# Conformer layer of a hybrid decoder trunk: opening in half groups, second product with three blocks side by side, modulation vectors dealt out anew

## The chip, the cores and the metric

The kernel runs on one core of a Trainium2 chip. A core has five engines that run side by side and each take their own instructions in order: TensorE (PE; its weight loads are shown as PEld), VectorE (DVE), ScalarE (ACT), GpSimd (POOL) and SyncE (SP), which here issues nearly all transfers. Sixteen DMA engines move data between HBM and the on-chip memory SBUF; TensorE writes its results to PSUM, of which the kernel has eight banks. The metric is the time of one execution on the device in microseconds; lower is better.

## What is computed

Two layers over 256 tokens of width 2048. Layer 0 mixes tokens with a causal Conformer convolution, layer 1 with a Mamba-2 scan; a squared-ReLU MLP of width 8192 follows each. Every sub-layer is normalised, scaled, shifted and gated by vectors that come from the conditioning vector c through w_mod. Cut to what matters:

```python
sc = jax.nn.silu(c)
for i in range(DEPTH):
    mod = (sc @ w_mod[i] + b_mod[i])[:, None, :]
    sh1, sc1, g1, sh2, sc2, g2 = jnp.split(mod, 6, axis=-1)
    u = rmsnorm(h, norm_mix_g[i]) * (1 + sc1) + sh1
    mix = conformer_conv(u, ...) if i % 2 == 0 else mamba2(u, ...)
    h = h + g1 * mix
    u = rmsnorm(h, norm_mlp_g[i]) * (1 + sc2) + sh2
    h = h + g2 * sq_relu_mlp(u, mlp_w1[i], mlp_w2[i])
return rmsnorm(h, final_norm_g)

def conformer_conv(u, ...):
    a, gt = jnp.split(u @ w_pw1 + b_pw1, 2, axis=-1)
    v = causal_dwconv(a * jax.nn.sigmoid(gt), w_dw, b_dw)      # 31 taps
    v = jax.nn.silu(layernorm(v, ln_g, ln_b))
    return v @ w_pw2 + b_pw2
```

## The kernel before

**Layout.** Activations lie transposed: 2048 channels are four groups of four tiles of 128 partitions, each 256 tokens wide. Weights come in tiles of 1 MB (`load_w`, tag `w32`, three buffers): 512 rows of one group by 512 output columns, a block. The first product of the Conformer (`native`, L632) uses float32 directly; all others go through `split_w` (L329 to L340), which makes of each half tile a high part on ACT (L337) and a low part on DVE (L338), three buffers each, and `products` (L342) sums high by high, high by low and low by high.

**Vectors of w_mod.** `mod` of a layer is 6 segments (SH1, SC1, G1, SH2, SC2, G2) of 16 column tiles. A job `(layer, segment, column tile)` is one `gemv` (L243): a 1 MB transfer into a buffer of tag `wm` (two) or `hid` (four), in the turn that `self.rings` gives, then a product with silu(c). For groups in `PE_GROUPS` this is done by TensorE (four matmuls, L258; after four jobs the row is copied by ACT, L264, and turned into columns by `columns`, L279), for the others by DVE in one pass (L267). `mod_done` adds the bias on POOL. `pump(n)` takes n jobs off the list; the tables `RATE_...` say how many at each weight tile. `need` takes whatever is still missing at once.

**Order.** The program is written in one order and a scheduler places each engine's instructions by priority (`high_priority(n)` moves them n places ahead). `issue_after(ins)` keeps what is traced in the block behind `ins` on the engine of `ins`. `stream` keeps all loads of weights and vectors on SP in the order of the program, so a load that waits for a buffer holds all later ones.

**Stages that the change touches.**
- *Opening* (`native` with the first three blocks, L618 to L676): the scale and shift of a group (eight vectors, all on DVE) must be there before its input `u` can be made (`vectors`, L538) and multiplied by three blocks.
- *First product, blocks 3 to 7*, beside the convolution (`conv`: 24 taps on ACT, L565, the rest on DVE; the last two channel tiles have 13 taps on TensorE, L576) and the sums of the LayerNorm (`close`, `moments`). Jobs run by `RATE_PW1`.
- *LayerNorm* (L707 to L748): last sums (L718), mean and variance, and `v`, the normed input in four groups. The first weight tile of the second product is split before it. Six jobs (`BETWEEN`) are given to TensorE behind the sums.
- *Second product* (L762 to L770): four blocks one after the other, each over all four groups (`block`); results go into h (`into_h`, L790, squares L499, sums L496). Then four jobs of (0, SC2, 2), moved to the front by `first`, are put on TensorE.
- *MLP of layer 0* (`mlp`, L811): `outer` takes three blocks side by side, group by group, while the modulated input of a group is made (`modulate`, L502), with jobs by `RATE_OPEN`.
- *MLP of layer 1*: the same opening without jobs; then one job at each weight tile, but `to_rows` (L861), stepped from the first `block`, needs all that are left (`need(1, G2)`), and then turns h into rows (L870, L871) in two buffers of tag `wm` and spreads the gate (L881, L882).

Of the kernel before, what the change touches and what calls it, by code (L numbers as in the profile page):

```python
# [29 lines left out]
def spread(n, slots):  # L30
# [128 lines left out]
class Trunk:  # L159
# [83 lines left out]
    def gemv(self, layer, seg, ct, parts=((0, 4),)):  # L243
# [8 lines left out]
        if (layer, seg, g) in PE_GROUPS:  # L252

            if i == 0:
                self.row_sums = self.bank(*self.side)
# [5 lines left out]
            if i == 3:  # L261
                row = self.t("t2", [P, 512], bufs=3)
                with self.tc.issue_after(self.act) if self.act else nullcontext():
# [3 lines left out]
        nc.vector.scalar_tensor_tensor(out=w, in0=w, scalar=1.0, in1=self.scb, op0=ALU.mult,  # L267
                                       op1=ALU.mult, accum_out=m[:, i:i + 1])
# [15 lines left out]
    def mod_done(self, layer, seg, kg, i0=0, i1=4):  # L284
# [3 lines left out]
        nc.gpsimd.tensor_tensor(out=m, in0=m, in1=self.col("b_mod", (layer * 6 + seg) * NT + 4 * kg + i0, n),  # L288
                                op=ALU.add)
        if seg in (SC1, SC2):  # L290
            g = "norm_mix_g" if seg == SC1 else "norm_mlp_g"
            nc.gpsimd.tensor_scalar(out=m, in0=m, scalar1=1.0, scalar2=1.0, op0=ALU.add, op1=ALU.mult)
            nc.gpsimd.tensor_tensor(out=m, in0=m, in1=self.col(g, layer * NT + 4 * kg + i0, n), op=ALU.mult)
# [20 lines left out]
    def first(self, layer, seg, g):  # L314

        take = lambda j: j[0] == layer and j[1] == seg and j[2] // 4 == g
        self.jobs = [j for j in self.jobs if take(j)] + [j for j in self.jobs if not take(j)]

# [10 lines left out]
    def split_w(self, w):  # L329

        nc = self.nc
        out = []
        for i in range(2):
            s = slice(2 * i, 2 * i + 2)
            wh = self.wp.tile([P, 2, 512], F32R, tag="wh", name=self.nm("wh"), bufs=3)
            wl = self.wp.tile([P, 2, 512], F32R, tag="wl", name=self.nm("wl"), bufs=3)
            nc.scalar.copy(out=wh, in_=w[:, s, :])  # L337
            nc.vector.tensor_tensor(out=wl, in0=w[:, s, :], in1=wh.bitcast(F32), op=ALU.subtract)  # L338
            out.append((wh, wl))
        return out  # L340
# [15 lines left out]
    def block(self, src, rhs, evac, pump=None, single=False, ahead=None, there=()):  # L356
# [5 lines left out]
        for g in range(4):  # L362
            w, parts = there[g] if g < len(there) else (self.load_w(src[g]), None)
            if pump:
                self.pump(pump(g))
            if parts is None:
                with self.tc.high_priority(self.ahead if ahead is None else ahead):
                    parts = self.split_w(w)
# [44 lines left out]
    def outer(self, srcs, make, evac, pump):  # L413

        banks = [[self.bank(self.mm, "mm") for _ in range(2)] for _ in srcs]
        for g in range(4):
            x = make(g)
            for b, src in enumerate(srcs):
                w = self.load_w(src[g])
                with self.tc.issue_after(self.split):  # L420
                    self.pump(pump(g))
                with self.tc.high_priority(self.ahead):
                    parts = self.split_w(w)
# [90 lines left out]
    def conformer(self):  # L514
# [12 lines left out]
        nc.vector.reciprocal(r, r)  # L527
# [29 lines left out]
        def conv(ct):  # L557
# [5 lines left out]
            def products(p4, k):  # L563
                for q in range(4):
                    nc.scalar.activation(out=p4[:, q, :], in_=vp[:, k + q:k + q + T], func=AF.Identity,  # L565
                                         scale=self.col("w_dw", ct * TAPS + k + q),
# [660 lines left out]
```

## Time and profile before

| | us |
|---|---|
| three runs | 2635.2, 2631.5, 2634.6 |
| median | 2634.6 |
| profiled execution | 2634.52 |
| its span | 2632.7 |

The profile is of one execution. The page lists each engine's busy time, the busy share in 40 slices, the DMA queues and the chain of waits that ended last; other views give busy time by stretch, groups of instructions by line, waits, and the timeline. A timeline row has the start, the busy time, the engine, the line, the operation, the output and inputs by the program's names, the shapes, the number of instructions merged (x), and in brackets the engine's idle time before it with what released it. A group's row has count, busy time and mean in ns, then the idle time before it. In rows of stretches stand the length, busy time and number of instructions of PE, weight load, DVE, ACT and POOL, the granted clock of TensorE as a share of full speed, the DMA share and GB/s. SPq is the queue of SP; its row is the issue, not the transfer. A float32 matmul is two instructions, a float32r one is one. Some 2 us of the profiled time lie outside the span.

### The profile page before, as it was taken

The page shows a single profiled execution, that of the slowest core. Times are in us where ns is not written, and L with a number is a line of the kernel's source. Part 1 is how long each engine was busy: PE and PEld are TensorE (multiplying, and loading weights), DVE is VectorE, ACT ScalarE, POOL GpSimd, SP SyncE. Part 2 cuts the span into 40 slices and gives each one's busy share as a digit, 9 for nine tenths or more (in the row PEclk, how much of TensorE's full clock was granted, in tenths as well). Part 3 has the DMA queues.
Part 4 walks back from the last instruction along what each step waited for, and adds up shares of the span by engine and source line. Part 5 has one row for each costly group of instructions (what it writes and reads, how often), then busy time and mean ns, then how long its engine had stood idle before and what let it go on. Part 6 is the DMA issues. An engine that isn't in the chain of part 4 may idle for free.

```text
span 2632.7 us, 37210 instructions
## 1 busy us (share of the span) xinstructions
PE 2556.5 (97%) x14667; PEld 2202.8 (84%) x14667; DVE 1974.8 (75%) x2630; ACT 1360.2 (52%) x2155; POOL 124.6 (5%) x182
## 2 busy tenths in 40 slices
PE   6999899999999999999999999999989999999998
PEld 4777697988888888888888888888988888888886
DVE  6589887787888889888877777898865565565565
ACT  2099653444444434447777767644444344443443
POOL 0000000000000000000000000000000101101000
PEclk8999999999999999999999999999999999999999
DMA  9865687888888888866554455777655555555553
GB/s 406 337 256 225 245 342 306 313 315 308 312 320 313 320 313 320 316 265 210 187 190 178 172 194 181 252 294 305 239 217 200 192 191 192 192 181 195 185 190 144
DMA packets 92881, 659.15 MB, mean 250 GB/s; under 512 B 10497, under 2 KB 10497, under 8 KB 14753
## 3 DMA queue, kind: packets, MB, share of 16 engines
q1 hardware_dynamic: 89138, 644.53, 64.6%
q0 software_dynamic: 3136, 10.59, 1.3%
q8 instruction: 115, 1.88, 0.3%
q10 hardware_dynamic: 432, 1.66, 0.2%
q14 instruction: 60, 0.49, 0.0%
HBM read 654.53 MB, written 2.20 MB: 249 GB/s over the span
## 4 chain that ended last, share of the span: by engine, by line
PE 93%; DVE 3%; DMA 2%; ACT 1%; issue 1%; POOL 0%; ACTq 0%; DVEq 0%; SPq 0%; POOLq 0%
PE mm L346 68%; PE mm L632 7%; PE mm L399 4%; PE mm L397 4%; PE mm L398 4%; DMA wm<-wmT 1%; PE ms L258 1%; DVE wm L267 1%; DMA hid<-wmT 1%; PE ms L1141 1%; DVE wl L338 1%; DVE hid L267 1%; PE mm L258 0%; PE ms L524 0%; PE ms L475 0%
## 5 line engine op out<-in xcount | busy, mean ns | idle before, releaser
L346 PE MATMUL mm<-u,wh 128*128 128x512 f32 (+1 forms) x4544 | 1371.7, 365 | 3.2 <-ACT wh L337 2.8
L337 ACT CAST wh<-w 128x1024 fp32r<-128x1024 f32 x768 | 806.6, 1051 | 1000.2 <-PE mm L346 721.2
L338 DVE TENSOR_TENSOR wl<-w,wh 128x1024 fp32r<-128x1024 f32 x768 | 940.8, 1229 | 471.6 <-ACT wh L337 467.7
L346 PE MATMUL mm<-u,wl 128*128 128x256 f32 x3840 | 1076.0, 282 | 3.5 <-DVE wl L338 3.4
L346 PEld LDWEIGHTS mm<-u,wh 128*128 128x128 f32 x4544 | 810.9, 190 | 151.4 <-issue 6.1
L346 PEld LDWEIGHTS mm<-u,wl 128*128 128x128 f32 x3840 | 728.3, 190 | 9.7 <-DVE wl L338 5.2
L346 PE MATMUL mm<-hid,wh 128*128 128x512 f32 (+1 forms) x1344 | 452.9, 387 | 2.8 <-DVE acc L807 2.8
L346 PE MATMUL mm<-hid,wl 128*128 128x256 f32 x1280 | 358.8, 281 | 0.0
L267 DVE SCALAR_TENSOR_TENSOR wm<-wm,scb 128x2048 f32<-128x2048 f32 x129 | 294.8, 2285 | 16.6 <-DMA wm<-wmT 16.4
L346 PEld LDWEIGHTS mm<-hid,wh 128*128 128x128 f32 x1344 | 248.9, 189 | 58.9 <-DVE acc L807 3.2
L632 PE MATMUL mm<-u,w 128*128 128x256 f32 x1024 | 231.7, 388 | 27.4 <-ACT u L545 25.8
L632 PEld LDWEIGHTS mm<-u,w 128*128 128x128 f32 x1024 | 197.2, 194 | 65.3 <-ACT u L545 27.2
L346 PEld LDWEIGHTS mm<-hid,wl 128*128 128x128 f32 x1280 | 242.5, 189 | 0.3 <-issue 0.2
L397 PE MATMUL mm<-wh,hid 128*128 128x512 f32 x512 | 199.9, 390 | 0.0
L399 PE MATMUL mm<-wh,hid 128*128 128x512 f32 x512 | 199.9, 390 | 0.0
L398 PE MATMUL mm<-wl,hid 128*128 128x512 f32 x512 | 199.5, 390 | 0.0
L565 ACT ACTIVATE taps<-u,par 128x256 f32<-128x256 f32 x360 | 148.4, 500 | 0.6 <-DVE u L554 0.6
L399 PEld LDWEIGHTS mm<-wh,hid 128*128 128x128 f32 x512 | 96.1, 188 | 19.8
L398 PEld LDWEIGHTS mm<-wl,hid 128*128 128x128 f32 x512 | 96.1, 188 | 19.6
L397 PEld LDWEIGHTS mm<-wh,hid 128*128 128x128 f32 x512 | 96.2, 188 | 19.5
L288 POOL TENSOR_TENSOR mod<-mod,par 128x4 f32<-128x4 f32 (+2 forms) x52 | 39.3, 755 | 1411.8 <-DVE wm L267 997.1
L580 DVE TENSOR_TENSOR taps<-taps,taps 128x1024 f32<-128x1024 f32 x74 | 90.4, 1221 | 8.1 <-ACT taps L565 7.3
(234 smaller groups left out, 1598.1 us busy)
## 6 DMA issues: line engine op xcount, KB each, us to landing
w<-w SPq DMA_DIRECT2D x256, 1024.0 KB, 4.8
wm<-wmT SPq DMA_DIRECT2D x140, 1024.0 KB, 7.0
w<-win SPq DMA_DIRECT2D x80, 1024.0 KB, 4.8
hid<-wmT SPq DMA_DIRECT2D x52, 1024.0 KB, 11.1
w<-pw SPq DMA_DIRECT2D x48, 1024.0 KB, 4.9
w<-wout SPq DMA_DIRECT2D x32, 1024.0 KB, 6.5
acc<-ac_d POOLq DMA_DIRECT2D x16, 512.0 KB, 6.9
h<-xT SPq DMA_DIRECT2D x4, 512.0 KB, 6.4
```

The lines of the kernel that those rows point to most:

```text
L258: self.pe = nc.tensor.matmul(self.row_sums[32 * t:32 * t + 32, :], lhsT=self.scol[:, kt:kt + 1].broadcast_to([P, 32]), rhs=w[:, t * 512:(t ...
L267: nc.vector.scalar_tensor_tensor(out=w, in0=w, scalar=1.0, in1=self.scb, op0=ALU.mult, op1=ALU.mult, accum_out=m[:, i:i + 1])
L288: nc.gpsimd.tensor_tensor(out=m, in0=m, in1=self.col("b_mod", (layer * 6 + seg) * NT + 4 * kg + i0, n), op=ALU.add)
L337: nc.scalar.copy(out=wh, in_=w[:, s, :])
L338: nc.vector.tensor_tensor(out=wl, in0=w[:, s, :], in1=wh.bitcast(F32), op=ALU.subtract)
L346: self.pe = self.nc.tensor.matmul(out, lhsT=lhsT, rhs=rhs, skip_group_check=True, **kw).ins
L397: mm(banks[q], lhsT=hi, rhs=wh[:, k, :], start=g == 0 and t == 0, stop=False)
L398: mm(banks[q], lhsT=hi, rhs=wl[:, k, :], start=False, stop=False)
L399: mm(banks[q], lhsT=lo, rhs=wh[:, k, :], start=False, stop=g == 3 and t == 3)
L565: nc.scalar.activation(out=p4[:, q, :], in_=vp[:, k + q:k + q + T], func=AF.Identity, scale=self.col("w_dw", ct * TAPS + k + q), bias=self ...
L580: nc.vector.tensor_add(wide, wide, products(four("wl"), k))
L632: self.pe = nc.tensor.matmul(o, lhsT=w[:, t, j * P:(j + 1) * P], rhs=u[g][:, t, :], start=g == 0 and t == 0 and j < 2, stop=g == 3 and t == 3,
```

## The change

- The opening works in half groups: after four vectors the first two tiles of a group are made and multiplied by all three blocks, then the other two. The weight tiles are loaded between the vectors. The reciprocal of the norm moves behind the fourth vector. For the last tiles of group 3 the bias (and scale) is put in by DVE instead of POOL.
- Jobs: 4 instead of 12 in the first product, 8 instead of 6 behind the sums, 24 instead of 16 and then 4 in the second product, 12 in the MLP's opening. The order is now scale and shift group by group; on TensorE are G1, (SC2, 0), (SH2, 0) and (SH2, 3). `first` and the four jobs behind the second product go. A new group on TensorE first turns older rows into columns.
- The second product takes three blocks side by side through `outer` and then the fourth; `normed(g)` makes each group of its input when `outer` comes to it. Of the first weight tile only one half is split ahead, its high part behind the last tap on ACT, its low part behind the last difference on DVE. The last square gets a higher priority, and the first difference of the normed input moves before the reciprocal. The bias goes into h at group 3.
- The MLP of layer 1 takes eight jobs in its opening (`RATE_LAST`). In `to_rows` four diagonals become one operation on DVE and one matmul.

```diff
-RATE_PW1 = spread(12, 20)
-BETWEEN = 6
-RATE_PW2 = [1, 1, 1, 1, 1, 1, 1, 1, 1, 1, 2, 1, 2, 1, 0, 0]
-CHANGE = (0, SC2, 2)
-RATE_OPEN = [1, 0, 1, 2, 2, 1, 1, 1, 1, 0, 1, 1]
+RATE_PW1 = spread(4, 20)
+BETWEEN = 8
+RATE_PW2 = [2, 2, 2, 2] + spread(16, 12)
+RATE_OPEN = [1, 1, 2, 1, 1, 2, 1, 2, 1, 0, 0, 0]
+RATE_LAST = spread(8, 12)
...
-EARLY = [(0, G1, g) for g in range(4)] + [
-    (0, SC2, 0), (0, SH2, 0), (0, SC2, 1), (0, SH2, 1), (0, SH2, 2), CHANGE, (0, SH2, 3), (0, SC2, 3)]
-
-PE_GROUPS = {(0, G1, g) for g in range(4)} | {(0, SC2, 0), CHANGE, (0, SH2, 3)}
+EARLY = [(0, G1, g) for g in range(4)] + [(0, s, g) for g in range(4) for s in (SC2, SH2)]
+
+PE_GROUPS = {(0, G1, g) for g in range(4)} | {(0, SC2, 0), (0, SH2, 0), (0, SH2, 3)}
...
+                while len(self.rows_left) > 1:
+                    self.columns()
...
+        if (layer, seg, kg) in ((0, SC1, 3), (0, SH1, 3)):
+            nc.vector.tensor_add(m, m, b)
+            if seg == SC1:
+                nc.vector.scalar_tensor_tensor(out=m, in0=m, scalar=1.0, in1=g, op0=ALU.add, op1=ALU.mult)
+            return
...
+    def split_half(self, w, i, hi_after=None, lo_after=None):
+        nc = self.nc
+        s = slice(2 * i, 2 * i + 2)
+        wh = self.wp.tile([P, 2, 512], F32R, tag="wh", name=self.nm("wh"), bufs=3)
+        wl = self.wp.tile([P, 2, 512], F32R, tag="wl", name=self.nm("wl"), bufs=3)
+        after = lambda v: self.tc.issue_after(v) if v else nullcontext()
+        with after(hi_after):
             nc.scalar.copy(out=wh, in_=w[:, s, :])
+        with after(lo_after):
             nc.vector.tensor_tensor(out=wl, in0=w[:, s, :], in1=wh.bitcast(F32), op=ALU.subtract)
-            out.append((wh, wl))
-        return out
+        return wh, wl
+
+    def split_w(self, w, done=()):
+
+        return list(done) + [self.split_half(w, i) for i in range(len(done), 2)]
...
+    def outer(self, srcs, make, evac, pump, there=()):
+
+
+        there = list(there)
         banks = [[self.bank(self.mm, "mm") for _ in range(2)] for _ in srcs]
         for g in range(4):
             x = make(g)
             for b, src in enumerate(srcs):
-                w = self.load_w(src[g])
+                w, done = there.pop(0) if there else (self.load_w(src[g]), ())
...
+            for g in range(4):
+                vec(g, 0)
+                vec(g, 1)
+                if g == 0:
+                    with self.tc.issue_after(self.sum):
+                        nc.vector.reciprocal(r, r)
+                vectors(g, 0, 2)
+                load(0, g)
+                vec(g, 2)
+                load(1, g)
+                if g < 3:
+                    vec(g, 3)
+                load(2, g)
                 for i in range(3):
-                    load(i, g)
-                    products(i, g, 0, 4)
-                    if i < 2:
-                        vec(g + 1, i)
-                if g < 2:
-                    for t in (2, 3):
-                        vec(g + 1, t)
-                    vectors(g + 1, 0, 4)
-            vectors(3, 0, 2)
-            vec(3, 2)
+                    products(i, g, 0, 2)
+                if g < 3:
+                    vectors(g, 2, 4)
+                    for i in range(3):
+                        products(i, g, 2, 4)
...
+        there = [self.load_w(a["pw2"][b, 0]) for b in range(3)]
...
+            root = nc.scalar.activation(out=var, in_=var, func=AF.Sqrt, bias=self.eps).ins
+            d = dd[0][:, 0, :]
+            nc.vector.tensor_sub(d, d, mean)
+            recip = nc.vector.reciprocal(var, var).ins
...
+        def normed(g):
+
+            with self.tc.high_priority(AHEAD_NORM if g else AHEAD_CHAIN):
                 vg = self.b("u", [P, 4, 2 * T], F32R)
                 if g:
-                    nc.vector.tensor_sub(dd[g], dd[g], wide(mean))
-                    nc.vector.tensor_mul(dd[g], dd[g], wide(var))
+                    with self.tc.issue_after(recip):
+                        nc.vector.tensor_sub(dd[g], dd[g], wide(mean))
+                        nc.vector.tensor_mul(dd[g], dd[g], wide(var))
...
+        normed(0)
+
+        with self.tc.high_priority(AHEAD_CHAIN):
+            half = self.split_half(there[0], 0, tap, d15)
...
-        self.first(*CHANGE)
-        with self.tc.issue_after(self.pe):
-            self.pump(4)
...
+        def make(g):
+            if g:
+                normed(g)
+            if g == 3:
+                with self.tc.issue_after(st["silu"]):
+                    nc.scalar.activation(out=self.t("rcol", [P, 2])[:, :1], in_=self.eps, func=AF.Sqrt)
+                self.need(0, G1)
+                for b in range(4):
+                    gb = self.t("gb", [P, 4], bufs=2)
+                    nc.gpsimd.tensor_tensor(out=gb, in0=gate(b), in1=self.col("b_pw2", 4 * b, 4), op=ALU.mult)
+                    for j in range(4):
+                        hj = self.h[b][:, j, :]
+                        nc.scalar.activation(out=hj, in_=hj, func=AF.Identity, bias=gb[:, j:j + 1])
+            return v[g]
+
+        into = [self.into_h(res, b, gate) for b in range(4)]
+        self.outer([a["pw2"][b] for b in range(3)], make, lambda b, j, parts: into[b](j, parts), pump,
+                   there=[(there[0], [half]), (there[1], ()), (there[2], ())])
+        self.block(a["pw2"][3], v, into[3], pump=pump, single=True)
+        return res["ss"]
...
+                dg = self.t("t2", [P, 4, P], bufs=3)
+                nc.vector.tensor_tensor(
+                    out=dg, in0=self.ident.rearrange("p (o k) -> p o k", o=1).broadcast_to([P, 4, P]),
+                    in1=m.rearrange("p (j o) -> p j o", o=1).broadcast_to([P, 4, P]), op=ALU.mult)
+                yield from lag(3)
+                nc.tensor.matmul(ps, lhsT=self.ones, rhs=dg.rearrange("p j k -> p (j k)"), start=True, stop=True)
...
-        self.mlp(1, ss, pump=lambda g: 1)
+        last = iter(RATE_LAST)
+        self.mlp(1, ss, pump=lambda g: 1, first=lambda g: next(last))
```

More of the change, by code (lines that the diff above doesn't have):

```diff
@@ L354, in products, with block @@
             mm(bank[:, T:], wl[:, k, cs], x[:, t, :T], start=False, stop=stop)
-    def block(self, src, rhs, evac, pump=None, single=False, ahead=None, there=()):
+    def block(self, src, rhs, evac, pump=None, single=False, ahead=None):
         banks = [self.bank(self.mm, "mm") for _ in range(4)]
@@ L754, in conformer @@
         rate = iter(RATE_PW2)
[L756 to L774 removed]
+        pump = lambda g: next(rate)
+        res = {"ss": []}
+        gate = lambda b: self.mod_tile(0, G1, b)
+        def make(g):
[17 more added lines that the diff above has]
+        return res["ss"]
     def into_h(self, st, b, gate, after=None):
@@ L878, in to_rows @@
                 m = self.mod_tile(1, G2, 2 * i + k)
-                for j in range(4):
-                    dg = self.t("diag", [P, P], bufs=1)
-                    nc.vector.tensor_scalar_mul(out=dg, in0=self.ident, scalar1=m[:, j:j + 1])
-                    nc.tensor.matmul(ps[:, j * P:(j + 1) * P], lhsT=self.ones, rhs=dg, start=True, stop=True)
-                    yield
+                dg = self.t("t2", [P, 4, P], bufs=3)
[4 more added lines that the diff above has]
+                nc.tensor.matmul(ps, lhsT=self.ones, rhs=dg.rearrange("p j k -> p (j k)"), start=True, stop=True)
+                yield
                 nc.scalar.copy(out=v[:, k, :], in_=ps)
```

92 lines of the change are left out of this document (27 added, 65 removed).

## The prediction

> **What bounds the kernel now.** I read the page first, then the busy times by stretch, the chain of waits, and last the timelines of the stretches in which TensorE idles.
>
> ```profile
> span 2632.7 us, 37210 instructions
> PE 2556.5 (97%) x14667; PEld 2202.8 (84%) x14667; DVE 1974.8 (75%) x2630; ACT 1360.2 (52%) x2155; POOL 124.6 (5%) x182
> ```
> ```profile
> 20.00:60.00 40.00, 21.07 (x84) 18.04 (x85) 33.63 (x34) 3.09 (x6) 1.40 (x7) 0.74 1.01 420
> 165.00:288.00 123.00, 123.00 (x627) 97.76 (x626) 117.43 (x184) 115.46 (x289) 2.75 (x4) 1.00 0.59 223
> 280.00:290.00 10.00, 10.00 (x51) 7.82 (x50) 5.65 (x12) 1.04 (x3) 0.00 (x0) 1.00 0.45 169
> 310.00:320.00 10.00, 6.79 (x40) 2.14 (x44) 8.75 (x17) 3.54 (x5) 0.00 (x0) 0.83 0.11 19
> 330.00:431.00 101.00, 98.70 (x793) 96.39 (x792) 80.14 (x97) 49.91 (x84) 6.21 (x12) 0.97 0.87 352
> 1960.00:1970.00 10.00, 2.79 (x18) 2.24 (x16) 7.93 (x12) 1.61 (x5) 0.00 (x0) 0.84 0.55 209
> 1970.00:1980.00 10.00, 7.74 (x35) 6.39 (x36) 6.62 (x7) 6.65 (x10) 0.20 (x1) 0.65 0.89 358
> ```
>
> Columns: length, then PE, weight load, DVE, ACT, POOL busy, granted clock, DMA share, GB/s. TensorE carries the end. Its idle 76 us and its slow clock lie in a few places: the opening (transfers at 420 GB/s, the DMA full), the LayerNorm near 310 to 330, the openings of the MLPs, and 1960 to 1976. The change touches all of them. Between 165 and 288 TensorE never idles; ACT is at 94% and has a hole of 9.0 us only at 280 to 290, where it waits for the last block.
>
> **Opening.** The page gives 1024 KB for each vector and weight, so 2.5 us each at 420 GB/s. A group of input rows is 8 vectors and 3 weights, 27.5 us.
>
> ```profile
> 12.73 2.29 DVE L267 SCALAR_TENSOR_TENSOR hid<-hid,scb 128x2048 f32<-128x2048 f32 x1 [5.78 <-DMA hid<-wmT]
> 21.32 1.75 DVE L527 RECIPROCAL t<-t 128x256 f32<-128x256 f32 x1 [3.88 <-ACT t L526]
> 38.93 45.07 PE L632 MATMUL mm<-u,w 128*128 128x256 f32 x192 [19.50 <-ACT u L545]
> 90.32 9.89 PE L632 MATMUL mm<-u,w 128*128 128x256 f32 x31 [6.32 <-ACT u L545]
> 136.57 7.14 PE mm L632 x32
> 100.46 14.14 SPq L322 DMA_DIRECT2D w<-pw  x3
> 90.00:100.00 10.00, 9.68 (x31) 8.07 (x32) 7.44 (x7) 1.57 (x4) 0.00 (x0) 0.69 1.01 421
> ```
>
> One block's group is 32 instructions, 7.1 us, so three blocks take 21.3 us. Group 2 started at 90.32, its last weight slot came free at 114.6, and group 3 ended 21 us later, near 135. With half groups TensorE can start after four vectors instead of eight: from 12.7 four times 2.3 us on DVE, the reciprocal (1.75), which now stands behind them instead of holding DVE for 3.9 us, and 0.9 for the first tile, so near 24.5 instead of 38.9, but then it runs behind the transfers: the third weight of group 0 is transfer 11, landing near 37, that of group 2 two groups later, near 92. Behind it lie half a group of one block and half of all three, 3.6 + 10.7 us, and some 2 us of slow clock: group 2 ends near 108, group 3 near 130. That is 5 us; the stop behind PE's slots on SP's queue (a weight of the next group is queued behind four vectors) may take some. I take -4; the ends are -8 (no slow clock) and +4.
>
> The slow clock is priced by the rows above: in the 10 us after a gap of 6.3 us the clock was 0.69, a loss of 3 us. Half groups leave a gap of about 4 us in each group (waiting for the third weight). The Trainium skill (TensorE: Matmul & The Clock Gate, "HAM oscillation — how this bites in real kernels") speaks against that: bursts that alternate with transfer waits above about 3.4 us start each burst at half rate. The 6.3 us gap here agrees; for gaps of 2 us no row shows a fall. By its 3.4 us at half rate a gap would cost 1.7 us, an estimate, a little over half of the row's 3, and the time would be 2614. A group has 6.2 us of slack against its transfers, so a loss of 3 us a group is mostly covered; where it isn't is the rival below.
>
> **First product.** RATE_PW1 puts 4 instead of 12 vectors there, all reduced on TensorE.
>
> ```profile
> 277.26 1.06 PE L258 MATMUL mm<-hid,scol 128*32 128x512 f32 x8
> 456.99 0.95 PE L279 MATMUL ms<-bT,t 128*128 128x1 f32 x8
> ```
>
> A vector costs 1.06 us of TensorE, a group's turn into columns 0.95. Eight vectors and two turns are 10.4 us less on the path, capped by ACT's hole of 9.0: -9 (end: -5.6, DVE's idle of 123.0 - 117.4).
>
> **LayerNorm.** Splits of the next weight sit in front of the last convolution on DVE and ACT:
>
> ```profile
> 302.74 1.22 DVE L338 TENSOR_TENSOR wl<-w,wh 128x1024 fp32r<-128x1024 f32 x1
> 306.88 1.23 DVE L338 TENSOR_TENSOR wl<-w,wh 128x1024 fp32r<-128x1024 f32 x1
> 312.49 1.05 ACT L337 CAST wh<-w 128x1024 fp32r<-128x1024 f32 x1 [5.33 <-DVE acc L601]
> 313.44 0.41 ACT L604 ACTIVATE nrm<-acc 128x256 f32<-128x256 f32 x1
> 313.90 0.48 PE L718 MATMUL mm<-nrm,ones 128*128 128x256 f32 x1 [0.70 <-ACT nrm L604]
> 318.06 0.33 SPq L322 DMA_DIRECT2D wm<-wmT  x1
> 325.99 1.08 PE L258 MATMUL ms<-wm,scol 128*32 128x512 f32 x4 [1.72 <-DMA wm<-wmT]
> 329.58 0.56 PE L346 MATMUL mm<-u,wh 128*128 128x256 f32 x1
> ```
>
> The edit puts the split's two halves behind the last tap and the last difference, and the square first: 1.22 + 1.23 + 0.95 = -3.3 (end: -1). The cast is only delayed; it and three more casts then have to fit beside the first products. After the sums (314.6) products start 15 us later, because TensorE's queue holds vectors whose loads wait for a buffer that TensorE's first vectors free (issued from 318.06). The vector at 325.99 is already the seventh. With 8 instead of 6 ahead of the products, the eighth lands 2.5 us later, near 328.5, and one more microsecond reduces it; before, a turn into columns (1.9 us at slow clock) stood in that place. So 0; ends -6 (products go ahead of the late vectors) and +3.
>
> **Second product.**
>
> ```profile
> 348.70 54.83 PE mm L346 x456
> 404.68 1.23 DVE wl L338
> 412.47 1.15 DVE wl L338
> L267 DVE SCALAR_TENSOR_TENSOR hid<-hid,scb 128x2048 f32<-128x2048 f32 x9 | 20.5, 2284 | 0.0
> L790 DVE SCALAR_TENSOR_TENSOR h<-mm,mod,h 128x256 f32<-128x256 f32 x16 | 7.4, 480 | 7.3 <-PE mm L346 7.3
> L496 DVE TENSOR_TENSOR ssum<-ssum,sq 128x256 f32<-128x256 f32 x12 | 5.0, 419 | 0.1
> L258 PE MATMUL ms<-hid,scol 128*32 128x512 f32 x10 | 2.1, 604 | 0.0
> L279 PE MATMUL ms<-bT,t 128*128 128x1 f32 x16 | 1.9, 240 | 0.0
> ```
>
> A matmul is 0.120 us here, a slot (one weight tile, 48 matmuls) 5.8 us; the 16 slots are unchanged. Before, TensorE reduced 1.25 vectors here (10 instructions) and 2 turns; now 12 vectors (the rest of G1, SC2 0, SH2 0) and 4 to 5 turns, 10.75 x 1.06 and 2.5 x 0.95: +14, so the first product's relief comes back here. Three blocks side by side need only the first normed group for 17 us instead of all four in 23; that takes small waits before 348.7: -2.
>
> DVE's vectors now stand closely: none in slots 0 to 6, 12 in slots 7 to 15 and 8 in the first six slots of the MLP's opening. From slot 7 to the opening's group 1 DVE has 30 splits (36.6), 20 vectors (45.6), evacuation (16 x 0.48 and 12 x 0.42: 12.7), one normed group (two operations of the split's width, four of the sums': 4.1) and three modulated ones (eight operations each like the 0.48: 11.5): 111 us. TensorE has 15 slots and the gap between the products, 94. Of the 17 us of excess six vector buffers let DVE lag by 6 x 2.28 = 13.7. I take +5 with the two waits at 404 and 412 (1.1 and 1.5 us) as the nearest rows; the ends are 0 and 17.
>
> **Openings of the MLPs.**
>
> ```profile
> 430.16 1.04 PE L258 MATMUL ms<-hid,scol 128*32 128x512 f32 x2
> 444.36 5.71 PE mm L346 x33
> 1869.90 9.25 PE mm L346 x77
> 1886.11 64.35 PE mm L346 x527
> 1950.49 16.41 SPq L322 DMA_DIRECT2D wm<-wmT  x4
> 1971.59 1.11 PE L870 MATMUL ms<-ident,h 128*128 128x128 f32 x4 [8.80 <-ACT wm L871]
> ```
>
> In layer 0 four vectors fill TensorE's queue between the products and stand in front of the norm's own matmuls; steady products return 14.2 us after 430.16. Layer 1, without them, needs 1879.2 to 1886.1, 6.9 us. Dropping `first` and `pump(4)`: -7 (end -4). In layer 1 the last vectors are all called for at once by `to_rows`, with two buffers: TensorE waits 8.8 us and has slow clock after it; 18 and 35 instructions against 86 in a full ten microseconds, less 4 us of transposes, make 12 us. RATE_LAST spreads eight vectors over the opening before, where DVE and DMA have room: -12 (end -9). One 512-wide product for four diagonals takes out three small products of a group and DVE's waits between them: -1, an estimate with 0 as its end, since DVE has room there.
>
> **Sum** against the profiled execution, 2634.5 us (span 2632.7; the median of the runs is 2634.6): -4 - 9 - 3.3 + 0 + 14 - 2 + 5 - 7 - 12 - 1 = -19.3, so 2615.
>
> **Rivals.**
> *Late loads in the second product (slower).* SP issues in order, and a vector that waits stops the weights behind it: at 310 to 320 the DMA moved 19 GB/s. In slots 0 to 3 each weight comes with two vectors that TensorE itself consumes, 7.5 us of transfer against 5.8 + 2.0 us of work, so it decides from a rate below 400 GB/s or a start that is late. Then each of 14 vectors (12 and the two more before) holds TensorE's queue for some 2 us, as 1.72 at 325.99: +28, 2643. Against it: 420 GB/s in the full stretches.
> *The bursts cost what they bring.* Gaps at half clock in the opening (+4 for -4) and DVE's excess half uncovered (+4 more): 2627. For it: the clock rows; against: the slack of 6.2 us a group.
> *Products go ahead of the late vectors*, -6 at the LayerNorm: 2609, with no DVE excess 2604. For it: one product did so before 325.99.
> *The spread vectors don't remove the wait in layer 1* (the last one lands late): 12 us stay, 2627.
>
> **Chances.** Forecast (2607 to 2623) 0.50; better 0.12; gains lost in the opening, on DVE or in layer 1 (2623 to 2634) 0.20; slower (2638 to 2650) 0.15; nothing 0.03. A run tells some 0.2%, 5.3 us, from no change: of the lost-gain case 0.06 lies within it. Faster 0.76, same 0.09, slower 0.15. The range, 2600 to 2638, leaves out part of the better and most of the slower case.
>
> **What would show it.** The first L632 near 24 us and block 3's start near 132; ACT's hole at the end of the first product nearly gone; no L338 between the last taps; L346 some 15 us after the sums; about 14 us more between there and the norm, of which 12 vectors at L258; 7 us between second product and MLP; no wait on L871's copies in layer 1. A second product more than 125 us long, or waits on wm and hid loads within it, would make the forecast wrong.

## The result and the profile after

The changed kernel takes 2640.4 us (median, 2632.4 to 2646.3), the kernel before 2633.9 us in the runs beside it: a ratio of 1.0026, 95% interval 1.0017 to 1.0035. It is slower by a quarter of a per cent, where 2615 us was forecast. The profiled execution took 2645.2 us, 4.8 more than the median; the one of before was 0.6 above its own. So the traces lie 10.8 us apart and the medians 6.5, and a part of what the marks below show is scatter. From the page after:

```profile
span 2643.5 us, 37156 instructions
PE 2563.7 (97%) x14643; PEld 2210.3 (84%) x14643; DVE 1973.1 (75%) x2627; ACT 1360.3 (51%) x2155; POOL 124.3 (5%) x182
```

The span is 10.8 us longer, and TensorE is busy 7.2 us longer with the same products, but for the merged diagonals (matmuls at slow clock count as busy). Where the time goes is read from marks that both timelines have. First the opening, PE's timeline after (start, busy time, and in brackets the wait):

```profile
25.61 9.89 PE L638 MATMUL mm<-u,w 128*128 128x256 f32 x32 [6.46 <-ACT u L549]
39.96 19.91 PE L638 MATMUL mm<-u,w 128*128 128x256 f32 x80 [4.46 <-ACT u L549]
61.99 3.72 PE L638 MATMUL mm<-u,w 128*128 128x256 f32 x16 [2.13 <-DMA w<-pw]
71.58 19.46 PE L638 MATMUL mm<-u,w 128*128 128x256 f32 x80 [5.86 <-ACT u L549]
94.58 5.41 PE L638 MATMUL mm<-u,w 128*128 128x256 f32 x16 [3.54 <-DMA w<-pw]
104.17 20.22 PE L638 MATMUL mm<-u,w 128*128 128x256 f32 x80 [4.18 <-ACT u L549]
128.49 20.01 PE L638 MATMUL mm<-u,w 128*128 128x256 f32 x80 [4.09 <-ACT u L549]
150.06 14.91 PE L638 MATMUL mm<-u,w 128*128 128x256 f32 x68 [1.56 <-DMA w<-pw]
```

TensorE does start 13.3 us earlier than before (38.93), and yet block 3 starts 13.5 us later (150.06 against 136.57). The modulated input (u) is late in every group, by 4.1 to 6.5 us, and the third weight in two, by 2.1 and 3.5; from one group's second half to the next (39.96 to 71.58) it is 31.6 us, not 27.5. Then, after, the stretch of the first product and rows of the timeline behind it:

```profile
150.00:288.00 138.00, 137.94 (x670) 116.67 (x673) 133.00 (x203) 137.33 (x344) 0.00 (x0) 1.00 0.52 193
```
```profile
316.04 1.06 PE L724 MATMUL mm<-nrm,ones 128*128 128x256 f32 x2
329.90 1.44 PE L350 MATMUL mm<-u,wh 128*128 128x256 f32 x5
456.54 0.58 PE L480 MATMUL ms<-ones,ssum 128*128 128x1 f32 x4 [1.78 <-DVE ssum L501]
```

ACT's hole at the end of the first product is gone (137.33 of 138 us busy): the vectors that left it did shorten the path. From the first steady product (329.90) to the sums of the MLP's norm (456.54; 431.14 before) it is 126.64 us, against 101.56. The first matmul on the MLP's hidden rows is the next mark, in the groups of the products' line, before and then after (x count: min/median/max ns, first to last start):

```profile
431.14 0.61 PE L475 MATMUL ms<-ones,ssum 128*128 128x1 f32 x4
```
```profile
L346 PE MATMUL mm<-hid,wh x1344: 278/395/793, 544.5 to 1787.9; 128*128 128x512 f32 x174, 128*128 128x256 f32 x18
```
```profile
L350 PE MATMUL mm<-hid,wh x1344: 281/395/797, 570.9 to 1815.5; 128*128 128x512 f32 x174, 128*128 128x256 f32 x18
```

And the last MLP's opening after, in the stretch from its first product to well past the place where its wait stood:

```profile
1912.00:2099.00 187.00, 187.00 (x1125) 166.96 (x1126) 124.12 (x154) 88.68 (x122) 13.68 (x8) 0.99 0.58 214
```

TensorE never idles there; the wait of 8.8 us on the copies is gone. Put together (us, difference after minus before, from the marks):

| stretch | forecast | measured |
|---|---|---|
| start to block 3 | -4 | +13.5 |
| block 3 to the LayerNorm's last sums | -12.3 | -11.0 |
| last sums to steady products | 0 | -2.2 |
| second product, to the norm's sums | +17 | +25.1 |
| norm's sums to the MLP's hidden products | -7 | +1.0 |
| all behind that | -13 | -15.6 |
| sum | -19.3 | +10.8 |

### The profile page after: what moved, and what is told of

Its sections match the earlier page's. It is cut to its first block, busy times and chain, and to the rows that moved or that the text cites. A ratio compares the mean times of both kernels' runs of the same rounds, so it can differ in the third digit from the quotient of the medians.

```text
span 2643.5 us, 37156 instructions
## 1 busy us (share of the span) xinstructions
PE 2563.7 (97%) x14643; PEld 2210.3 (84%) x14643; DVE 1973.1 (75%) x2627; ACT 1360.3 (51%) x2155; POOL 124.3 (5%) x182
## 4 chain that ended last, share of the span: by engine, by line
PE 86%; DVE 5%; ACT 4%; DMA 3%; issue 1%; POOL 0%; SPq 0%; ACTq 0%; DVEq 0%
PE mm L350 66%; PE mm L401 4%; PE mm L400 4%; PE mm L402 4%; ACT taps L569 3%; PE mm L638 3%; DMA hid<-wmT 2%; DVE taps L585 1%; DVE wl L339 1%; PE ms L259 1%; DMA wm<-wmT 1%; DVE taps L588 1%; DVE hid L268 1%; DMA t<-eac_d 1%; DVE wm L268 0%
## 5 line engine op out<-in xcount | busy, mean ns | idle before, releaser
L638 PE MATMUL mm<-u,w 128*128 128x256 f32 x1024 | 238.8, 397 | 32.3 <-ACT u L549 25.1
L638 PEld LDWEIGHTS mm<-u,w 128*128 128x128 f32 x1024 | 203.2, 200 | 69.4 <-ACT u L549 27.1
L400 PE MATMUL mm<-wh,hid 128*128 128x512 f32 x512 | 200.8, 392 | 0.0
L268 DVE SCALAR_TENSOR_TENSOR hid<-hid,scb 128x2048 f32<-128x2048 f32 x35 | 80.1, 2288 | 31.6 <-DMA hid<-wmT 31.4
L296 POOL TENSOR_TENSOR mod<-mod,par 128x4 f32<-128x4 f32 (+1 forms) x52 | 37.8, 726 | 1373.1 <-DVE wm L268 931.5
```

The source lines that it names most:

```text
L268: self.sum = nc.vector.scalar_tensor_tensor(out=w, in0=w, scalar=1.0, in1=self.scb, op0=ALU.mult, op1=ALU.mult, accum_out=m[:, i:i + 1]).ins
L296: nc.gpsimd.tensor_tensor(out=m, in0=m, in1=b, op=ALU.add)
L400: mm(banks[q], lhsT=hi, rhs=wh[:, k, :], start=g == 0 and t == 0, stop=False)
L638: self.pe = nc.tensor.matmul(o, lhsT=w[:, t, j * P:(j + 1) * P], rhs=u[g][:, t, :], start=g == 0 and t == 0 and j < 2, stop=g == 3 and t == 3,
```

## Experiments

Each is timed in five rounds beside the kernel before, which took 2632.7, 2633.3 and 2633.6 us in the three groups of runs; a difference between kernels of two groups carries about 1 us from that alone. The theories' letters are those of the expectations: A is that the new opening loses by its order, S that the new shares of the vectors do.

**The opening of before put back** (in the kernel after):

```
-            for g in range(4):
-                vec(g, 0)
-                vec(g, 1)
...
+            for t in range(4):
+                vec(0, t)
+            vectors(0, 0, 4)
+            for g in range(3):
...
```

> The changed kernel with the opening of before (whole groups, the vectors of the next group loaded between the weights of this one, reciprocal before the vectors, bias by POOL). Theory A (the half groups hold each weight tile over both halves, and the vectors queued behind the weights on SP come late, 31 to 32 us a group): block 3 starts near 136.6 us instead of 150.1, and since ACT is full from there to 288 all later work moves with it: 13 us less, 2627. Rival (the later start costs nothing because the convolution's chain on ACT and DVE sets the end of that stage anyway): the first product of the second matrix stays near 330 and the time near 2640.

Measured 2625.6 us, ratio 0.9968 (0.9957 to 0.9979): 14.8 us less than after.

```profile
135.85 14.91 PE L634 MATMUL mm<-u,w 128*128 128x256 f32 x68 [1.41 <-DMA w<-pw]
```

Block 3 starts where it did before, and what follows keeps its length up to the MLP: from the first steady product to the hidden rows it is 241.0 us in both.

**The half groups alone** (the kernel before with the opening of after):

> The kernel before with the opening in half groups alone. Theory A: block 3 starts near 150 instead of 136.6; TensorE is full from there to 290, so the end moves by 13 us: 2647. Rival: part of it is caught up in the first product, under 5 us left: 2637 to 2639.

Measured 2647.1 us, 1.0052 (1.0039 to 1.0064), 14.4 us more than the kernel before beside it; block 3 starts at 147.52. The loss belongs to the opening and doesn't need the rest of the change.

**The last MLP alone** (the kernel before with these lines, and one product for four diagonals):

```
+RATE_LAST = spread(8, 12)
...
-        self.mlp(1, ss, pump=lambda g: 1)
+        last = iter(RATE_LAST)
+        self.mlp(1, ss, pump=lambda g: 1, first=lambda g: next(last))
```

> The kernel before with the last opening alone (vectors by RATE_LAST, four diagonals as one). The two traces put that stretch 15.6 us shorter in the changed kernel. Expected: the wait of 8.8 us before the transposes gone, 15 us less, 2619. Rival (the stretch is shorter only because eight vectors instead of six were left and other work moved): under 8 us less, above 2626.

Measured 2619.8 us, 0.9949 (0.9936 to 0.9961): 12.9 us less than the kernel before beside it, the largest gain of one part, by the smallest edit. The spread vectors and the merged diagonals were not timed apart.

**The old shares** (in the kernel after, the three blocks side by side kept):

```
-RATE_PW1 = spread(4, 20)
-BETWEEN = 8
-RATE_PW2 = [2, 2, 2, 2] + spread(16, 12)
+RATE_PW1 = spread(12, 20)
+BETWEEN = 6
+RATE_PW2 = [1, 1, 1, 1, 1, 1, 1, 1, 1, 1, 2, 1, 2, 1, 0, 0]
...
+        self.first(*CHANGE)
+        with self.tc.issue_after(self.pe):
+            self.pump(4)
```

(and RATE_OPEN, EARLY and PE_GROUPS of before.)

> The changed kernel with the old shares of the vectors in layer 0 (12 in the first product, 6 behind the sums, 16 and 4 in and behind the second product, old order and old groups on TensorE), the second product still three blocks side by side. Theory S (the new shares make the loss: 12 vectors on TensorE and then DVE's vectors in a row in front of the splits): from the first product of the second matrix (L350) to the norm's sums it takes 103 to 106 us instead of 124.8, the MLP's opening 60 instead of 67, the first product some 10 us longer: 2624. Rival O (the order of three blocks side by side, with the normed groups made between, makes the loss): that stretch stays above 115 us, and with the longer first product the time is 2645 or more.

Measured 2621.1 us, 0.9959 (0.9945 to 0.9972): 19.4 us less than after, so the loss in the second product comes with the shares. The order of the products isn't at fault: with the old shares it brings the norm's sums 104.0 us after the first product (330.1 to 434.14), and the hidden rows 108.1 us later, 113.4 before.

**Opening and shares both of before**, so that the side-by-side order, the LayerNorm's edits and the last MLP remain:

> The changed kernel with both the opening and the shares of before: what is left of the change is the second product with three blocks side by side, the LayerNorm's late split and early square, and the last opening. If the two losses are separate, the opening gives back what block 3's start shows (144.7 in the run with old shares, 136 with the old opening): 2621 - 9 = 2612. If they overlap (the full DMA of the one hides the other), it stays near 2619.

Measured 2610.6 us, 0.9915 (0.9901 to 0.9928): faster than both kernels, and 9.1 us faster than the last MLP's edit alone. So the remaining edits gain. By the marks of the two traces 3.6 us of it lie between block 3 and the LayerNorm's last sums, and 5.3 between the norm's sums and the hidden rows. The opening gives back 10.4 us here, against 14.8 in the kernel after; with the old shares the half groups brought block 3 to 144.74.

**Vectors ahead of weights in the half groups** (in the kernel after; from group 1 on the vectors of the second half are asked for before the group's weights):

```
                 vectors(g, 0, 2)
+                if g:
+                    vec(g, 2)
+                if g in (1, 2):
+                    vec(g, 3)
                 load(0, g)
-                vec(g, 2)
+                if not g:
+                    vec(g, 2)
                 load(1, g)
```

> The changed kernel, and in its opening the vectors of a group's second half are asked for ahead of its weights from group 1 on; the half groups stay. Theory A (vectors queued on SP behind weights that wait for a slot): the DMA no longer runs empty while the slots are held, a group takes 27.5 to 29 us instead of 31 to 33, block 3 starts at 137 to 140 and the time is 2628 to 2631. Rival (the bursts at half clock and the slots themselves make the loss, whatever the order): block 3 starts after 146 and the time is above 2636.

Measured 2623.7 us, 0.9961 (0.9948 to 0.9975): 16.7 us less than after, by an order of issues alone, and 4 us below the range of theory A. First SP's queue in the kernel after (start of the issue), its longest waits from 20 to 160 us (total, times, longest), and the stretches 100 to 140 us:

```profile
80.71 0.33 SPq L323 DMA_DIRECT2D w<-pw  x1
...
87.62 0.33 SPq L323 DMA_DIRECT2D w<-pw  x1
...
94.41 0.33 SPq L323 DMA_DIRECT2D hid<-wmT  x1
114.06 0.33 SPq L323 DMA_DIRECT2D w<-pw  x1
114.52 0.35 SPq L323 DMA_DIRECT2D hid<-wmT  x1
```
```profile
SPq L323 <- PE mm L638: 100.9, 13, 22.7
```
```profile
100.00:120.00 20.00, 15.83 (x61) 13.47 (x62) 13.56 (x17) 1.81 (x4) 0.37 (x2) 0.83 0.78 311
120.00:140.00 20.00, 15.90 (x63) 13.28 (x62) 11.03 (x16) 2.06 (x3) 0.00 (x0) 0.83 0.66 276
```

From 94.41 to 114.06 SP issues nothing: the first weight of the next group waits until TensorE lets its slot go, and half groups hold a weight through both halves. The vectors of the second half stand behind that weight, so the DMA runs partly empty (0.78 and 0.66 busy) while the vectors that TensorE will wait for are not yet asked for. The same shows earlier: in the four stretches of 20 us from 20 to 100 the DMA share is 1.01, 0.78, 0.93 and 0.90 in the kernel after, and 1.01 or 1.02 in each both in the kernel before and with the vectors ahead. With the vectors ahead, the waits, the same stretches and block 3's start are:

```profile
SPq L323 <- PE mm L638: 77.6, 15, 15.1
```
```profile
100.00:120.00 20.00, 20.00 (x94) 17.60 (x94) 12.03 (x20) 1.42 (x3) 0.00 (x0) 1.00 0.94 373
120.00:140.00 20.00, 18.43 (x86) 15.94 (x85) 11.73 (x18) 12.72 (x29) 0.00 (x0) 1.00 0.47 177
```
```profile
134.14 14.91 PE L638 MATMUL mm<-u,w 128*128 128x256 f32 x68 [1.57 <-DMA w<-pw]
```

TensorE is busy throughout 100 to 120 at full clock, block 3 starts 15.9 us earlier, and at 120 the loads are nearly done.

**Other groups on TensorE** (the opening of before; which groups of the second product's vectors TensorE reduces):

```
-PE_GROUPS = {(0, G1, g) for g in range(4)} | {(0, SC2, 0), (0, SH2, 0), (0, SH2, 3)}
+PE_GROUPS = {(0, G1, g) for g in range(4)} | {(0, SC2, 1), (0, SC2, 2), (0, SH2, 3)}
```

> The changed kernel with the opening of before, and (0, SC2, 1) and (0, SC2, 2) on TensorE in place of (0, SC2, 0) and (0, SH2, 0): the same numbers of vectors on each engine and the same tables, only DVE's vectors start in slot 2 of the second product instead of slot 7. The run with the opening of before needs 200.8 us from the first L345 of the second product to the end of the MLP's opening (315.6 to 516.4), the kernel before 175. Theory D (DVE's vectors come in a row and stand in front of the splits): 185 to 190 us, time 2610 to 2616. Rival P (the work of 12 vectors on TensorE and the transfers are the price, whoever reduces when): above 196 us, time 2621 or more.

Measured 2623.6 us, 0.9963 (0.9951 to 0.9976), 2.0 less than with the opening of before alone, and their intervals overlap. That VectorE's vectors stand bunched is not the price.

The next three start from the kernel with the opening of before (2625.6 us) and ask what in the shares costs.

**VectorE's reductions shortened:**

```
+        n = 128 if layer == 0 and seg in (SC2, SH2) else D
+        self.sum = nc.vector.scalar_tensor_tensor(out=w[:, :n], in0=w[:, :n], scalar=1.0, in1=self.scb[:, :n],
```

> The kernel after with the opening of before, in which VectorE reduces only 128 of 2048 columns of its 20 vectors of layer 0's SC2 and SH2 (it leaves out most of that reduction; the loads stay whole). The stretch from the first product of the second pointwise product to the long run of the first MLP took 200.8 us with the same opening and whole reductions, 172.2 us with the old shares. Theory D (VectorE's time for these vectors, 20 x 2.28 = 45.6 us, is what makes TensorE wait): the stretch falls to 185 us or less and the time to 2610 us or less. Theory T (the transfers, 1.33 vectors and one weight a slot, set the pace): the stretch stays at 196 us or more and the time at 2621 us or more. Theory N (the eight vectors more that stand there cost their own TensorE time): as T, since TensorE's share is unchanged.

Measured 2610.4 us, 0.9916 (0.9903 to 0.9930): 15.2 us less, as much as the old shares give.

**Half the transfers, VectorE's time kept:**

```
+        half = layer == 0 and seg in (SC2, SH2) and (layer, seg, g) not in PE_GROUPS
+        n = D // 2 if half else D
+        self.stream(w[:, :n], self.a["wmT"][layer, seg, ct][:, :n])
...
+        for _ in range(2 if half else 1):
```

> The same kernel, in which VectorE's 20 vectors of layer 0's SC2 and SH2 load only half their columns, and VectorE reduces that half twice (it leaves out the other half of the reduction): VectorE's time as before, 10 MB or 25 us of transfers less. Theory T (transfers): the stretch from the second product to the long run of the MLP falls by 10 us or more from 200.8 us, the time to 2615 us or less. Theory D (VectorE's time): the stretch stays at 196 us or more, the time at 2621 us or more. If both this kernel and the one with light reductions stay where they were, neither VectorE nor the transfers set the pace, and TensorE's own share does.

Measured 2620.1 us, 0.9947 (0.9935 to 0.9960): 5.6 us less.

**Only the eight vectors back in the first product:**

```
-RATE_PW1 = spread(4, 20)
+RATE_PW1 = spread(12, 20)
-RATE_PW2 = [2, 2, 2, 2] + spread(16, 12)
+RATE_PW2 = [1, 1, 1, 1, 1, 1, 1, 1, 1, 1, 2, 1, 2, 1, 0, 0]
```

> The kernel after with the opening of before (2625.6 us) in which only the eight vectors that the change moved out of the first product go back there: 12 instead of 4 in the first product, and the rates of before in the second product; the new order of the vectors, which groups TensorE reduces and the rates at the MLP's openings stay. Theory N (the number of vectors in the second product is the price): the stretch from the second product to the long run of the MLP falls from 200.8 to about 178 us, the first product grows by 8 us, and the time is 2611 us (2607 to 2615). Theory B (the order of the vectors, SC2 and SH2 by turns in full groups on VectorE, is the price): the stretch stays above 192 us, and the time is 2621 us or more.

Measured 2618.3 us, 0.9947 (0.9934 to 0.9959): 7.3 us less, half of what all the old shares give (15.0: 2625.6 to 2610.6). The norm's sums of the four kernels, in the order opening of before, light reductions, half loads, eight vectors back:

```profile
442.21 0.58 PE L475 MATMUL ms<-ones,ssum 128*128 128x1 f32 x4 [1.78 <-DVE ssum L496]
```
```profile
429.06 0.58 PE L476 MATMUL ms<-ones,ssum 128*128 128x1 f32 x4
```
```profile
427.69 0.58 PE L478 MATMUL ms<-ones,ssum 128*128 128x1 f32 x4 [0.49 <-DVE ssum L499]
```
```profile
431.63 0.58 PE L475 MATMUL ms<-ones,ssum 128*128 128x1 f32 x4 [0.45 <-DVE ssum L496]
```

Steady products start at 315.6, 311.2, 314.4 and 320.7 us, and the hidden rows at 556.6, 537.9, 545.1 and 543.0. So:

| kernel | second product | to the hidden rows | both |
|---|---|---|---|
| opening of before | 126.6 | 114.4 | 241.0 |
| light reductions | 117.9 | 108.8 | 226.7 |
| half loads | 113.3 | 117.4 | 230.7 |
| eight vectors back | 110.9 | 111.4 | 222.3 |
| old shares too | 104.3 | 108.1 | 212.4 |

Neither pure theory holds. By the mark of the expectations, the start of the long run of the MLP, the stretch of 200.8 us becomes 186.5 with light reductions, 189.3 with half loads, 180.8 with the eight vectors back and 172.4 with the old shares too. Light reductions miss the bounds that VectorE's time set by 1.5 us of the stretch and 0.4 of the time, and they shorten both parts. Half loads meet the stretch that the transfers set and miss their time by 5 us; they take every wait over 0.5 us out of the second product and make the MLP's opening 3 us longer, with a wait of 4.4 us on its input. The eight vectors back come near the stretch of theory N and miss its range of time by 3 us. TensorE's own share of the eight vectors, 8 x 1.06 + 2 x 0.95 = 10.4 us, is less than the 15.7 by which the second product shrinks without them. So each of the three takes some of the waits away, and the account that fits all of them is that the new shares fill TensorE, VectorE and the transfers in the same slots. The runs don't separate two things: a short reduction also gives its buffer back 2 us earlier, and half loads come with a reduction in two pieces of 1.22 us, between which VectorE can do a split.

Single profiles scatter. The steady products of the first three kernels start between 311.2 and 315.6 us, though their programs are the same up to there. From the hidden rows' first matmul to their last the same work took 1239 to 1246 us; half loads shorten the stretch by 10.3 us and the time by 5.6, and 6.2 us are lost in that work (1245.5 against 1239.3), for a reason that stays open.

What those waits are is seen in the kernel after, by window (300 to 440 and 440 to 570; total us, times, longest):

```profile
PE mm L350 <- DVE wl L339: 4.7, 3, 3.9
PE mm L350 <- ACT wh L337: 3.2, 1, 3.2
```
```profile
PE mm L350 <- DVE wl L339: 2.5, 1, 2.5
PE mm L350 <- ACT u L457: 2.3, 2, 1.2
...
PE ms L480 <- DVE ssum L501: 1.8, 1, 1.8
```

The longest, 3.9 us, ends on a split's low half. VectorE's timeline ahead of it:

```profile
430.32 2.28 DVE L268 SCALAR_TENSOR_TENSOR wm<-wm,scb 128x2048 f32<-128x2048 f32 x1
...
432.53 0.42 DVE L501 TENSOR_TENSOR ssum<-ssum,sq 128x256 f32<-128x256 f32 x1
432.87 2.28 DVE L268 SCALAR_TENSOR_TENSOR hid<-hid,scb 128x2048 f32<-128x2048 f32 x1
...
435.08 0.42 DVE L501 TENSOR_TENSOR ssum<-ssum,sq 128x256 f32<-128x256 f32 x1
435.42 2.35 DVE L339 TENSOR_TENSOR wl<-w,wh 128x1024 fp32r<-128x1024 f32 x2
```

Two vectors and the evacuation's sums, 5.1 us, stand in front of a split that TensorE is waiting for. A wait of the same kind and length (3.90 us) stands in the second product with the old shares too, at 406.41 us with opening and shares of before, so this one alone is not the difference. The wait of 3.2 us on a cast is less direct. VectorE, ACT and PE:

```profile
407.32 2.28 DVE L268 SCALAR_TENSOR_TENSOR wm<-wm,scb 128x2048 f32<-128x2048 f32 x1
...
409.53 1.26 DVE L808 SCALAR_TENSOR_TENSOR h<-mm,mod,h 128x256 f32<-128x256 f32 x3
```
```profile
410.04 0.42 ACT L504 ACTIVATE sq<-h 128x256 f32<-128x256 f32 x1 [2.19 <-DVE h L808]
410.37 1.98 ACT L337 CAST wh<-w 128x1024 fp32r<-128x1024 f32 x2
```
```profile
411.45 0.74 PE L350 MATMUL mm<-u,wh 128*128 128x256 f32 x4 [3.21 <-ACT wh L337]
```

The cast stands on ACT behind a square of the evacuation, the square waits for h, and VectorE makes this h only after a vector. None of ACT's waits from 300 to 460 ends on a load, so no weight was late. How much of the 3.2 us the vector makes was not tested. In the kernel with half loads both waits are absent.

**The best parts together** (old shares, side-by-side order, spread at the last MLP, and the half groups with their vectors ahead of the weights):

> The old shares of the vectors, the three blocks side by side and the spread at the last MLP (2610.6 us with the opening of before), now with the opening in half groups in which each half's vectors are asked for ahead of the group's weights. That opening brought block 3 to 134.1 us in the kernel after, against 135.85 with the opening of before. Theory A (the order on SP's queue was the whole loss of the opening): block 3 starts near 134, so 1 to 2 us are won: 2609 us (2606 to 2612). Rival (half groups cost something of their own with the old shares): 2615 us or more.

Measured 2609.6 us, 0.9909 (0.9896 to 0.9923); block 3 starts at 133.10. Its runs (2609.0 to 2611.0) overlap with those of the same kernel with the opening of before (2609.7 to 2612.2): the half groups, put right, move block 3 by 2.7 us, and the time no more than can be told. Both beat the kernel before by 0.9%.

## Why the prediction was wrong

*The opening: the term that failed most.* The step "-4; the ends are -8 (no slow clock) and +4" put the stop on SP's queue at "may take some": it saw a weight behind four vectors and not the vectors of the second half behind a weight whose slot is held over both halves. The start near 24.5 was right (25.61); the third weight of group 2, said to land near 92, ended a wait at 94.58, but the second half of group 3's vectors was not asked for before 114.52. The term measured +13.5 in this trace; the same half groups measured +11.0 alone and +8.2 with the old shares (block 3 at 147.52 and 144.74), all above the end of +4. The runs on the opening show it: alone it costs 14.4 us, put back it returns 14.8 (10.4 with the old shares), reordered it returns 16.7. The slow clock of the bursts that the text weighed is there (0.78 to 0.91 in the stretches of 20 us from 20 to 140), but it follows from the waits and doesn't by itself account for the loss: with the vectors ahead it is nearly as low up to 100 us (0.81 to 0.93) and full from there, and block 3 starts earlier than in the kernel before.

*VectorE's excess: mis-sized.* "I take +5", with ends of 0 and 17. Where most of VectorE's reductions of these vectors are left out, the time falls by 15.2 us, near the upper end. All waits of these stages and the clock behind them are more: 126.6 - 113.3 = 13.3 us of the second product are gone in the kernel with half loads, and the MLP's opening behind the gap, from the first steady product to the hidden rows, grew by 7.0 (444.36 to 544.5 before, 463.80 to 570.9 after). That is 20 instead of 5, VectorE's share and that of the transfers together. The excess of 17 us of VectorE's work was counted as if six buffers could hide most of it, and the transfers were not counted in the same slots. TensorE's own part of the second product, +12 forecast, came out at 113.3 - 101.6 = 11.8 (unrounded) in the kernel with half loads. That is partly luck: the side-by-side order was to take 2 us off this stretch, and with the old shares it is 104.0 and 104.3 us long, 2 to 3 more than before, a wait of 3.90 us among them.

*The gap at the MLP's norm: right in size, the mechanism not borne out.* The forecast of -7 came from dropping `first` and `pump(4)`. From the norm's sums to the first steady product it was 13.2 us before (431.14 to 444.36); after, and with the old shares, steady products start at

```profile
463.80 1.10 PE L350 MATMUL mm<-u,wh 128*128 128x256 f32 x3 [1.24 <-ACT u L457]
```
```profile
443.08 0.39 PE L358 MATMUL mm<-u,wl 128*128 128x256 f32 x1 [0.53 <-DVE wl L347]
```

which is 7.3 and 8.9 us (434.14 to 443.08). But the run with the old shares has `first` and the four jobs back: they stand in the gap as before, and 4.3 of the 6.0 us are won all the same, because TensorE's waits of 2.41 and 1.09 us on the first split are 0.34 and 0.53 there and the clock is full. What shortened them was not followed up.

*Right in size:* the first product with the LayerNorm's edits (-11.0 for -12.3; the LayerNorm's edits -3.6 for -3.3 without the rest), the start of the second (-2.2 for 0), and the last MLP (-15.6 for -13; -12.9 alone).

*The rivals.* "Late loads in the second product", 2643, has the measured time and the wrong cause: TensorE's waits for vectors' loads amount to 2.2 us, all ahead of the second product, and neither TensorE nor ACT waits for a weight in it. "The bursts cost what they bring" named both places that failed and gave them 12 us over the forecast, where they took some 33 (17.5 in the opening, 16 behind the LayerNorm). The list of signs was sound: block 3's start (150.06 for 132) was on it, and the length of the second product (126.6, bound 125) was named as deciding; both came out on the wrong side.

## What to carry to other kernels

On a queue that issues in order, sort loads by when their buffer comes free, not by when their data is used: a load that waits for a buffer stops every load behind it, and splitting work into halves lengthens the time for which the shared operand holds its buffer. When work is moved into another stage, add up TensorE, VectorE and transfers for the same slots: in a stage in which all are nearly full TensorE waits whenever one of them is late, and here each wait of 3 us or more brought slow clock on top. Undo a combined change part by part: here two of its parts hid a gain of 0.9% in the others.

## What the runs showed of the hardware

The slow clock after a wait did not always begin with the restart. PE's stretches of 2 us in the kernel after, behind the wait of 3.21 us that ended at 411.45, then the one of 4.46 us that ended at 39.96, then the one of 2.13 us that ended at 61.99:

```profile
411.00:413.00 2.00, 1.03 (x6) 0.83 (x7) 1.70 (x3) 2.00 (x5) 0.00 (x0) 1.00 0.36 152
413.00:415.00 2.00, 2.00 (x13) 2.00 (x13) 2.00 (x3) 0.90 (x1) 0.00 (x0) 0.61 0.08 25
415.00:417.00 2.00, 2.00 (x12) 2.00 (x11) 1.67 (x3) 0.40 (x1) 0.00 (x0) 0.54 0.93 365
417.00:419.00 2.00, 2.00 (x19) 2.00 (x19) 0.59 (x2) 0.71 (x2) 0.00 (x0) 1.00 0.97 406
```
```profile
40.00:42.00 2.00, 2.00 (x5) 1.64 (x6) 1.72 (x1) 0.31 (x1) 0.00 (x0) 0.50 1.01 422
42.00:44.00 2.00, 2.00 (x7) 1.55 (x6) 1.81 (x3) 0.00 (x0) 0.00 (x0) 0.50 1.04 426
44.00:46.00 2.00, 2.00 (x9) 1.70 (x8) 1.82 (x3) 0.00 (x0) 0.00 (x0) 0.80 0.92 377
...
62.00:64.00 2.00, 2.00 (x9) 1.79 (x10) 0.00 (x0) 0.00 (x0) 0.00 (x0) 1.00 1.01 426
```

After 3.21 us the clock stayed full until 413 and was then half for 2 x (0.39 + 0.46) / 0.5 = 3.4 us, 1.7 us lost; after 4.46 us it was half at once, for 4.8 us; after 2.13 us nothing was lost. The Trainium skill (TensorE: Matmul & The Clock Gate, "What's actually happening") says that the clock is set by how busy TensorE was in a window of about 3.4 us, which runs freely and does not start anew with the kernel; the late start and the 3.4 us of the first case agree with that. The waits of 3.54 us (ended at 94.58) and 3.89 us (at 436.69) went the same way: the clock of the stretches behind them was 1.00, 0.50, 0.65 (from 94) and 0.83, 0.50, 0.82 (from 436), 1.7 us lost in each. So the waits of 3.2 to 3.9 us cost about half as much again, and it is charged to matmuls that wait for nothing.
